# Two tables of weight sums instead of three in the second MLP of a decoder trunk, with the fourth block added on VectorE

## The chip, the core and the metric

The kernel runs on one core of one Trainium2 chip. The metric is the time of one execution on the device in microseconds (us), the median over runs. All data is float32 in memory. TensorE multiplies float32 data here as pairs of float32r halves ("hi" and "lo", three products for each float32 product), so every weight block first goes through ScalarE (the hi half, a copy to float32r) and VectorE (the lo half, what the copy left over).

Names of the engines as in the profile: PE is TensorE, PEld its weight loads, ACT is ScalarE, DVE is VectorE, POOL is GpSimd, SP is SyncE. SP and POOL here do almost nothing but issue DMA transfers; a transfer that adds to what stands at its target (an "accumulation" below) is issued by POOL in this kernel.

## The reference, cut to what matters

Two layers over 512 tokens of width 1024. Layer 0 is attention (16 heads) and an MLP, layer 1 a gated short convolution and an MLP. The MLP is the part the change works on:

```python
def conv_ffn(h, norm_g, w_up, conv_w, w_down):
    xn = rms_norm(h, norm_g)
    u = causal_dwconv(xn @ w_up, conv_w)          # w_up: 1024 x 5632
    g, val = u[..., :D_FF], u[..., D_FF:]         # D_FF = 2816
    return (jax.nn.silu(g) * val) @ w_down

def reference(x, ...):
    h = x
    for layer in range(2):
        mixer = attention_mixer if layer % 2 == 0 else short_conv_mixer
        h = h + mixer(h, ...)
        h = h + conv_ffn(h, ffn_norm[layer], ffn_w_up[layer], ffn_conv[layer], ffn_w_down[layer])
    return h
```

## The kernel before, in words

The program runs in stages, one after another on PE: attention, its output projection, the first MLP (up, then down), the input projection of the convolution mixer, its output projection, the second MLP (up, then down).

**Seven products instead of eight.** Most of the up projections and the input projection of the convolution are done as 2x2 block products in seven products rather than eight (`Sevens`). The weight of a group `g` of 256 columns is cut into four blocks of 512 rows: lower or upper half of the rows, gate or value columns. The seven products are named `p1 p7 p3 p6 p2 q5 q4`, and each of them takes one block or a sum of blocks as its weight. One product is 24 matmuls of 256 columns (`seven`). `slot(g, s)` issues slot `s` of group `g`: one product on PE, and around it the weight halves on ACT and DVE (`weights_of`), the loads for later slots on SP (`load_pair`, `load_one`), the accumulations on POOL (`add_block`). `p1` takes the block `X`; after its halves are made, `first_sums` lets POOL add another block to `X` in place, and `q5` takes that sum. `p2` takes the block `W`, `p3` the block `Z`, `p7` the buffer `Y`.

**Tables.** In the two MLPs three of the weights are sums over two, three and four blocks. They are not summed on chip: `table_steps` writes them beforehand as tables `t` in device memory. A table `7` is one block plus a second, a table `6` is table `7` plus a third, a table `4` is table `6` plus the fourth. Nine groups are cut into three pieces (`CHUNKS`), each piece into two halves of its rows; for each half the steps run copy, add, copy, add, copy, add, each of 768 KB. That is 36 transfers for a layer, all issued by POOL. An add waits for the copy before it, a copy from table to table waits for the add before it, and such a wait stands on POOL: whatever is behind it in POOL's queue stands too. The line of the adds is L101, that of the copies L104. `Y` is loaded from table `7`, `p6` takes table `6` and `q4` table `4`.

The list of 36 steps is a generator that the program draws from at fixed places; `FAR` says how many steps are drawn where. The order on POOL is the program's (`pin`). For layer 1: 9 steps behind the attention, 9 ahead of the convolution's first `first_sums`, 18 behind its slot 20 (the last accumulation into `Xc` is in that slot). A tile name with a `c` at its end (`Xc`, `Yc`) belongs to the convolution's seven products, which use accumulations instead of tables.

**Plain part and chores.** In each up projection groups 0 and 1 (`PLAIN = 2`) are done as plain products with 512 columns, and group 2 (`base`) is the first one of the seven-product form. What is left of the plain groups and of the preparation of the inputs is put into a list of chores for DVE and ACT; `up.rate` says how many microseconds of it (by the program's own estimate) are let go in a slot.

The instructions of PE, ACT and DVE are put in order by a scheduler in the framework; loads with a table, the halves on ACT and all transfers on POOL are held in the program's order.

Of the kernel before, what the change touches and what calls it, by code (L numbers as in the profile page):

```python
# [22 lines left out]
ALU = mybir.AluOpType  # L23
# [23 lines left out]
FILL1, FILL2, BEFORE = 1.5, 3.3, 2.0  # L47
UNITS = (0, 1), (2,), (3,)
PLAIN = 2
FAR = 9, 9, 18  # L50
CHUNKS = (2, 3), (5, 3), (8, 3)
SHARE = 0.58

# [2 lines left out]
def trunk(  # L56
# [7 lines left out]
    act, dve, pe, pool = nc.scalar, nc.vector, nc.tensor, nc.gpsimd  # L64
# [12 lines left out]
    def bank(tag):  # L77
        n_ps[0] += 1
        return ps.tile([P, S], F32, tag=tag, name=f"ps{tag}{n_ps[0]}", bufs={"a": 2, "b": 4, "c": 2}[tag])
# [6 lines left out]
    def table_steps(layer):  # L86

        w = ffn_w_up[layer]
        for n in "764":
            for g, m in CHUNKS:  # L90
                tables[layer, n, g] = far.tile([512, m * 256 + 16], F32, tag=f"t{layer}{n}{g}", name=f"t{layer}{n}{g}")
        def block(kh, half, g, m):
            return w[kh * 512:(kh + 1) * 512, half * DFF + g * 256:half * DFF + (g + m) * 256]
        for g, m in CHUNKS:
            for rows in (slice(0, 256), slice(256, 512)):
                for step in range(6):
                    n = "764"[step // 2]
                    to = tables[layer, n, g][rows, 0:m * 256]
                    if step % 2:
                        src = block(*((0, 1), (0, 0), (1, 0))[step // 2], g, m)  # L100
                        pin(nc.gpsimd.dma_start(to, src[rows, :], accum_op=ALU.add))  # L101
                    else:
                        src = block(1, 1, g, m) if step == 0 else tables[layer, "76"[step // 2 - 1], g][:, 0:m * 256]
                        pin(nc.gpsimd.dma_start(to, src[rows, :]))  # L104
                    yield

    def table_of(layer, n, group):
        g, m = next(c for c in CHUNKS if c[0] <= group < c[0] + c[1])
        return tables[layer, n, g][:, (group - g) * 256:(group - g + 1) * 256].rearrange("(k p) c -> p k c", p=P)
# [197 lines left out]
    def weights(ahead=AHEAD):  # L307
        fetch(1 + ahead)
        at[0] += 1
        return ready[at[0] - 1]  # L310
# [23 lines left out]
    class Norm:  # L334
# [3 lines left out]
        def __init__(self, name, base):  # L338
            self.name, self.base = name, base
            self.row, self.held, self.first = None, [], True  # L340
            self.acc = own.tile([P, S], F32, tag="nrow", name=f"nacc_{name}", bufs=1) if name != "n0" else None
# [135 lines left out]
    def products(acc, w, order=tuple(range(ND))):  # L477
        for k in order:
            yield mm3(acc, (w[0][:, k, :], w[1][:, k, :]), hs(k), k == order[0], k == order[-1])
# [486 lines left out]

    run(sums_far)
    sums_far = table_steps(1)

    def sum_far(n):  # L970
        for _ in range(n):
            next(sums_far, None)

    sum_far(FAR[0])

# [84 lines left out]
    class Sevens:  # L1060

        def __init__(self, name, mp, groups, block_of):
            self.name, self.mp, self.groups, self.block_of = name, mp, groups, block_of
            self.forms = {n: [mp.tile([P, 4, HT], F32R, tag=f"{n}_{i}", name=f"{n}_{i}{name}") for i in ("hi", "lo")] for n in FORMS}
            self.st, self.wides, self.table = {}, {}, None

        def load_pair(self, g):
            s = self.st[g] = {}
# [40 lines left out]
        def first_sums(self, g):  # L1109
            self.weights_of(g, "p7", "Y")  # L1110
            if not self.table:
                dve.tensor_tensor(self.st[g]["Y"], self.st[g]["Y"], self.st[g]["X"], op=ALU.add)
            self.add_block(g, "X", 0, 1)
            if self.table:
                self.load_one(g, "p6 sum", self.table("6", g))

        def open_wides(self, g):
            self.wides[g] = self.wides_of(g)
# [7 lines left out]
        def slot(self, g, s):  # L1126

            on, was, soon = (i in self.groups for i in (g, g - 1, g + 1))
            if self.chores:
                self.work_off(self.rate(g, s))  # L1130
            form, n, fresh = (("p1", "A", True), ("p7", "T", True), ("p3", "R", False), ("p6", "R", False), ("p2", "A", False),
                              ("q5", "R", False), ("q4", "T", False))[s]
            if s == 2:
                if was:
                    self.product(g - 1, form, n, fresh)
            elif on:
                self.product(g, form, n, fresh)
            st, p, c = self.st, g - 1, self.st.get(g)
            if s == 0:
                if was:  # L1140
                    if "p3" not in st[p]:
                        self.weights_of(p, "p3", "Z")
                    self.join(p, "yg", st[p]["T"], st[p]["Xs"])
                if on:
                    self.load_one(g, "W", self.block_of(g, 1, 0))
                if soon:
                    self.load_pair(g + 1)
            elif s == 1:
                first = not was
                if on and first and not self.ahead:  # L1150
                    self.weights_of(g, "p6", "p6 sum" if self.table else "Y")
                if on:
                    act.activation(self.bank_of(g, "R"), c["A"], AF.Copy, scale=-1.0)
                if on and not first:
                    self.weights_of(g, "p6", "p6 sum" if self.table else "Y")
                if soon and not self.table:
                    self.add_block(g + 1, "Y", 1, 1)
            elif s == 2:
                if on:
                    self.kept(g, "P7s", c["T"])  # L1160
                    self.weights_of(g, "p2", "W")
                    if self.table:
                        self.load_one(g, "q4 sum", self.table("4", g))
                    else:
                        dve.tensor_tensor(c["Y"], c["Y"], c["W"], op=ALU.add)
            elif s == 3:
                if was:
                    self.early(p, st[p]["R"])
                if on:
                    self.weights_of(g, "q5", "X")  # L1170
            elif s == 4:
                if on:
                    self.kept(g, "Xs", c["R"])
                    self.weights_of(g, "q4", "q4 sum" if self.table else "Y")
            if was and s != 2:
                self.tail(p, s)
            if s == 5:
                if on:
                    self.load_one(g, "Z", self.block_of(g, 1, 1))
                    self.open_wides(g)  # L1180
                    self.left(g, c["A"])
                if soon:
                    self.weights_of(g + 1, "p1", "X")
                elif on and self.ahead:
                    self.weights_of(g, "p3", "Z")
            elif s == 6:
                if on:
                    self.join(g, "yv", c["R"], c["P7s"])
                if soon:
                    self.first_sums(g + 1)  # L1190
# [17 lines left out]
    def up_seven(layer, norm, mp):  # L1208

        blocks = Blocks(mp, layer)  # L1210
        w_up, base = ffn_w_up[layer], PLAIN
# [5 lines left out]
        up = Sevens(layer, mp, range(base, HF), block_of)  # L1217
        up.norm, up.chores = norm, []
        up.table = lambda n, g: table_of(layer, n, g)
        up.rate = lambda g, s: 1.4 if g == base else 0.5  # L1220

        def wides_of(g):
            if g == base - 1:
# [78 lines left out]
    def conv_seven(norm, mp):  # L1302
# [5 lines left out]
        up = Sevens("c", mp, range(1, 5), block_of)  # L1308
# [98 lines left out]
        def gate(o, acc):  # L1407
            dve.tensor_tensor(early_b[:, o, :], acc, norm.row, op=ALU.mult)
            yield 0.69

        accs = []
        for j in range(8):
            accs.append(bank("bbbbaabb"[j]))
            for _ in products(accs[-1], weights(), (4, 5, 6, 7, 0, 1, 2, 3)):
                up.work_off(SHARE)
            if j in (1, 3):
                chores.append(input_(j // 2, *accs[j - 1:]))
            if j == 3:
                chores.append(prepare())
            if j >= 4:  # L1420
                chores.insert(0, gate(j - 4, accs[j]))
            if j == 5:
                up.load_pair(1)
                up.add_block(1, "Y", 1, 1)
                sum_far(FAR[1])
            if j == 7:
                up.weights_of(1, "p1", "X")
                up.first_sums(1)
                up.weights_of(1, "p6", "Y")
        want_conv_out()  # L1430
        for s in range(28):
            up.slot(1 + s // 7, s % 7)
            if s == 20:
                sum_far(FAR[2])
            if s == 27:
                fetch(1)
# [251 lines left out]
```

## Time and profile before

| what | value |
|---|---|
| three runs, us | 1143.35, 1142.93, 1141.8 (median 1142.93) |
| profiled execution, us | 1142.31, its span 1140.5 |
| PE busy | 1117.3 us (98% of the span), 7691 matmuls |
| DVE busy | 932.6 us (82%), ACT 679.0 us (60%), POOL 167.9 us (15%) |
| DMA | 223.51 MB, mean 196 GB/s |

The profiled execution took 0.62 us less than the median of the three runs, and 1.8 us of its time lie outside its span. PE is busy nearly everywhere, so a change can bring time only where PE stands still or where its clock is lowered, and cost time only where it makes PE stand. Shares of the whole span say little: what counts is, for each product, which of its operands came last, and whether PE had to wait for it. In us from the start of the span, the attention's last matmuls start at 255, the seven-product groups of the first MLP run on PE from 324 to 513, those of the convolution from 662 to 744, those of the second MLP from 834 to 1034, each behind its plain part, and the second MLP's down projection ends the program.

### The profile page before, as it was taken

The page shows a single profiled execution, that of the slowest core. Times are in us where ns is not written, and L with a number is a line of the kernel's source. Part 1 is how long each engine was busy: PE and PEld are TensorE (multiplying, and loading weights), DVE is VectorE, ACT ScalarE, POOL GpSimd, SP SyncE. Part 2 cuts the span into 40 slices and gives each one's busy share as a digit, 9 for nine tenths or more (in the row PEclk, how much of TensorE's full clock was granted, in tenths as well). Part 3 has the DMA queues.
Part 4 walks back from the last instruction along what each step waited for, and adds up shares of the span by engine and source line. Part 5 has one row for each costly group of instructions (what it writes and reads, how often), then busy time and mean ns, then how long its engine had stood idle before and what let it go on. Part 6 is the DMA issues. An engine that isn't in the chain of part 4 may idle for free.

```text
span 1140.5 us, 19427 instructions
## 1 busy us (share of the span) xinstructions
PE 1117.3 (98%) x7691; PEld 1010.5 (89%) x7691; DVE 932.6 (82%) x1430; ACT 679.0 (60%) x1013; POOL 167.9 (15%) x203
## 2 busy tenths in 40 slices
PE   8999999999999999999999999999969999999998
PEld 7888787878889999999999799988869999998886
DVE  6787888887889887888978988865968788788886
ACT  7556676745567666676556354543545666666553
POOL 4011111111011110024201111111111110014300
PEclk9999999999999999999999999999989999999999
DMA  6678778677888786799957967689886968799961
GB/s 192 180 173 205 164 182 200 162 204 194 214 213 213 194 215 179 198 315 195 225 158 181 233 151 159 143 228 235 241 185 178 220 173 211 204 251 228 230 158 56
DMA packets 182940, 223.51 MB, mean 196 GB/s; under 512 B 7900, under 2 KB 145164, under 8 KB 182848
## 3 DMA queue, kind: packets, MB, share of 16 engines
q0 software_dynamic: 43520, 96.38, 42.5%
q1 hardware_dynamic: 139168, 125.81, 35.5%
q8 instruction: 60, 0.98, 0.3%
q14 instruction: 32, 0.26, 0.1%
q10 hardware_dynamic: 160, 0.07, 0.0%
HBM read 217.26 MB, written 58.72 MB: 242 GB/s over the span
## 4 chain that ended last, share of the span: by engine, by line
PE 71%; DMA 12%; DVE 9%; issue 4%; ACT 3%; POOL 0%; DVEq 0%; SPq 0%; ACTq 0%; POOLq 0%
PE psb L1055 22%; PE psb L1600 10%; PE psa L1055 8%; PE psa L1600 8%; DMA t<-in_ffn_w_up 5%; PE psb L314 3%; PE psb L315 3%; PE psb L316 3%; DMA t<-t 2%; DMA Xc<-in_conv_w_in 2%; DMA X<-in_ffn_w_up 2%; PE psb L689 1%; PE psa L785 1%; PE psa L314 1%; PE psa L316 1%
## 5 line engine op out<-in xcount | busy, mean ns | idle before, releaser
L293 ACT ACTIVATE whi<-raw 128x1024 fp32r<-128x1024 f32 (+2 forms) x89 | 91.6, 1031 | 94.4 <-PE psb L315 26.0
L294 DVE TENSOR_TENSOR wlo<-raw,whi 128x1024 fp32r<-128x1024 f32 (+2 forms) x89 | 105.5, 1186 | 26.3 <-ACT whi L293 25.4
L1055 PE MATMUL psb<-p_lo,whi_p 128*128 128x256 f32 x432 | 121.6, 281 | 0.0
L1055 PE MATMUL psb<-p_hi,wlo_p 128*128 128x256 f32 x432 | 121.6, 281 | 0.0
L1055 PE MATMUL psb<-p_hi,whi_p 128*128 128x256 f32 x432 | 121.2, 281 | 0.0
L314 PE MATMUL psb<-hs_a,whi 128*128 128x512 f32 x224 | 92.2, 412 | 0.0
L1055 PE MATMUL psb<-q_hi,whi_q 128*128 128x256 f32 x288 | 81.2, 282 | 10.5 <-ACT Xs L1107 10.5
L316 PE MATMUL psb<-hs_a,wlo 128*128 128x512 f32 x224 | 88.7, 397 | 0.0
L1055 PEld LDWEIGHTS psb<-p_hi,whi_p 128*128 128x128 f32 x432 | 81.9, 190 | 0.0
L1055 PE MATMUL psa<-p_hi,wlo_p 128*128 128x256 f32 x288 | 81.9, 284 | 0.0
L1055 PE MATMUL psa<-p_lo,whi_p 128*128 128x256 f32 x288 | 81.8, 284 | 0.0
L1055 PE MATMUL psa<-p_hi,whi_p 128*128 128x256 f32 x288 | 81.6, 283 | 0.0
L1055 PEld LDWEIGHTS psb<-p_lo,whi_p 128*128 128x128 f32 x432 | 81.3, 188 | 0.0
L1055 PEld LDWEIGHTS psb<-p_hi,wlo_p 128*128 128x128 f32 x432 | 81.2, 188 | 0.0
L1055 PE MATMUL psb<-q_lo,whi_q 128*128 128x256 f32 x288 | 81.2, 282 | 0.0
L1055 PE MATMUL psb<-q_hi,wlo_q 128*128 128x256 f32 x288 | 81.0, 281 | 0.0
L101 POOL DMA_DIRECT2D t<-in_ffn_w_up x36 | 33.0, 916 | 222.0 <-DMA t<-t 121.9
L1055 PEld LDWEIGHTS psb<-q_hi,whi_q 128*128 128x128 f32 x288 | 54.7, 190 | 10.9 <-ACT Xs L1107 10.9
L1600 PE MATMUL psb<-act,whi 128*128 128x256 f32 x352 | 63.1, 282 | 0.1
L424 DVE SCALAR_TENSOR_TENSOR uv<-yv,taps,uv 128x511 f32<-128x511 f32 (+1 forms) x80 | 56.6, 745 | 0.0
L1600 PE MATMUL psb<-whi,act 128*128 128x512 f32 x176 | 56.3, 397 | 0.0
L424 DVE SCALAR_TENSOR_TENSOR ug<-yg,taps,ug 128x511 f32<-128x511 f32 (+1 forms) x80 | 55.6, 746 | 0.0
(475 smaller groups left out, 3644.8 us busy)
## 6 DMA issues: line engine op xcount, KB each, us to landing
t<-in_ffn_w_up POOLq DMA_DIRECT2D x48, 768.0 KB, 8.3
t<-t POOLq DMA_DIRECT2D x24, 768.0 KB, 5.0
raw<-in_attn_w_in SPq DMA_DIRECT2D x24, 512.0 KB, 5.1
X<-in_ffn_w_up SPq DMA_DIRECT2D x18, 512.0 KB, 5.1
Y<-t SPq DMA_DIRECT2D x18, 512.0 KB, 6.2
p6 sum<-t SPq DMA_DIRECT2D x18, 512.0 KB, 3.9
W<-in_ffn_w_up SPq DMA_DIRECT2D x18, 512.0 KB, 4.1
q4 sum<-t SPq DMA_DIRECT2D x18, 512.0 KB, 5.7
```

What stands on the lines that cost most here:

```text
L101: pin(nc.gpsimd.dma_start(to, src[rows, :], accum_op=ALU.add))
L293: return (act.activation(hi[:, at_], raw[:, at_], AF.Copy), dve.tensor_tensor(lo[:, at_], raw[:, at_], f32(hi[:, at_]), op=ALU.subtract))
L294: dve.tensor_tensor(lo[:, at_], raw[:, at_], f32(hi[:, at_]), op=ALU.subtract))
L314: made = [pe.matmul(acc, w[0], rhs[0], start=first, stop=False), pe.matmul(acc, w[0], rhs[1], start=False, stop=False), pe.matmul(acc, w[1 ...
L315: pe.matmul(acc, w[0], rhs[1], start=False, stop=False),
L316: pe.matmul(acc, w[1], rhs[0], start=False, stop=last)]
L424: dve.scalar_tensor_tensor(dst[:, d:], src[:, 0:S - d], tap(j), dst[:, d:], op0=ALU.mult, op1=ALU.add)
L689: pe.matmul(ss[e][:, c:c + wide], ql[rows, b * P:n], kl[rows, 0:wide], start=first and b == bs[0], stop=last and b == bs[-1])
L785: pe.matmul(out_, w, t[:, first:first + step * (NB - k - 1) + 1:step, :], start=k == 0 and i == 0, stop=k == NB - 1 and i == 1)
L1055: pe.matmul(to, w[a][:, k, c], x[b][:, k, :], start=fresh and i + k + t == 0, stop=i == 1 and k == 3 and t == 2, skip_group_check=not fresh)
L1600: pe.matmul(to, l, r, start=begin and o + t == 0, stop=end and t == 2 and o == (0 if layer else 1), skip_group_check=not fresh)
```

## The change

In layer 1 the table `4` is not written: 24 transfers stand in place of 36, and the nine loads of 512 KB from that table on SP go too. The sum of four blocks is made on DVE, in slot 2 of each group, as table `6`'s block (now named `three`) plus `W`, in place. The draws are placed anew: 7 steps behind the attention, one each behind slots 1, 8 and 15 of the convolution (right behind the accumulation into the next group's `Yc`), 14 behind slot 20. The rate of chores in the second MLP's groups behind the first is 0.3 instead of 0.5. Layer 0 keeps its three tables.

```diff
-FAR = 9, 9, 18
+FAR = 7, 1, 14
 ...
-        for n in "764":
+        for n in "76" if layer else "764":
 ...
-                for step in range(6):
+                for step in range(4 if layer else 6):
 ...
             if self.table:
-                self.load_one(g, "p6 sum", self.table("6", g))
+                self.load_one(g, "three", self.table("6", g))
 ...
                 if on:
                     self.kept(g, "P7s", c["T"])
                     self.weights_of(g, "p2", "W")
-                    if self.table:
-                        self.load_one(g, "q4 sum", self.table("4", g))
+                    if self.fours:
+                        self.load_one(g, "four", self.table("4", g))
                     else:
-                        dve.tensor_tensor(c["Y"], c["Y"], c["W"], op=ALU.add)
+                        c["four"] = c["three" if self.table else "Y"]
+                        dve.tensor_tensor(c["four"], c["four"], c["W"], op=ALU.add)
 ...
-        up.rate = lambda g, s: 1.4 if g == base else 0.5
+        up.fours = layer == 0
+        up.rate = lambda g, s: 1.4 if g == base else 0.3 if layer else 0.5
 ...
             if j == 5:
                 up.load_pair(1)
                 up.add_block(1, "Y", 1, 1)
-                sum_far(FAR[1])
 ...
         for s in range(28):
             up.slot(1 + s // 7, s % 7)
-            if s == 20:
+            if s in (1, 8, 15):
+                sum_far(FAR[1])
+            elif s == 20:
                 sum_far(FAR[2])
```

POOL's queue in the convolution's input projection, before (`Yc` and `Xc` are accumulations into the buffers of the weights, `t` are table steps):

```order
L1082 DMA Yc_7655<-in_conv_w_in 128x4x256
L101 DMA t_3286<-in_ffn_w_up 256x768
L104 DMA t_3289<-t_3286 256x768
L101 DMA t_3289<-in_ffn_w_up 256x768
L104 DMA t_3284<-in_ffn_w_up 256x768
L101 DMA t_3284<-in_ffn_w_up 256x768
L104 DMA t_3287<-t_3284 256x768
L101 DMA t_3287<-in_ffn_w_up 256x768
L104 DMA t_3290<-t_3287 256x768
L101 DMA t_3290<-in_ffn_w_up 256x768
L1082 DMA Xc_7654<-in_conv_w_in 128x4x256
```

The same place with the change:

```order
L1082 DMA Yc_7650<-in_conv_w_in 128x4x256
L1082 DMA Xc_7649<-in_conv_w_in 128x4x256
L1082 DMA Yc_7762<-in_conv_w_in 128x4x256
L101 DMA t_3286<-in_ffn_w_up 256x768
L1082 DMA Xc_7761<-in_conv_w_in 128x4x256
L1082 DMA Yc_7957<-in_conv_w_in 128x4x256
L104 DMA t_3284<-in_ffn_w_up 256x768
L1082 DMA Xc_7956<-in_conv_w_in 128x4x256
L1082 DMA Yc_8191<-in_conv_w_in 128x4x256
L101 DMA t_3284<-in_ffn_w_up 256x768
L1082 DMA Xc_8190<-in_conv_w_in 128x4x256
```

Nine table steps in a row ahead of the first `Xc` became single ones behind the `Yc` of groups 2, 3 and 4. Behind the last `Xc` there follow 18 steps before and 14 now, and then the second MLP's first accumulation into `X`.

DVE in group 2 of the second MLP, before (`p6 sum` is table 6's block, `whi` and `wlo` are the halves of a weight, `hs_a_wide` and `head` belong to chores):

```order
L1005 TENSOR_TENSOR wlo_p_9414<-p6 sum_9340,whi_p_9413 128x1024
L1042 TENSOR_TENSOR head_8980<-ug_9107,uv_9108 128x256
L1043 SCALAR_TENSOR_TENSOR head_8980<-ug_9107,uv_9108 128x256
L1271 TENSOR_TENSOR hs_a_wide_9431<-psb_9227,nrow_n_9085 128x512
L1271 TENSOR_TENSOR hs_a_wide_9431<-psc_9271,nrow_n_9085 128x512
L1271 TENSOR_TENSOR hs_a_wide_9431<-psc_9306,nrow_n_9085 128x512
L424 SCALAR_TENSOR_TENSOR hs_a_wide_9431<-hs_a_wide_9431,taps 128x511 x2
L424 SCALAR_TENSOR_TENSOR hs_a_wide_9431<-hs_a_wide_9431,taps 128x510 x2
L1005 TENSOR_TENSOR wlo_p_9422<-W_9379,whi_p_9421 128x1024
L1005 TENSOR_TENSOR wlo_q_9458<-X_9267,whi_q_9457 128x1024
```

The same place with the change:

```order
L1005 TENSOR_TENSOR wlo_p_9399<-three_9325,whi_p_9398 128x1024
L1042 TENSOR_TENSOR head_8965<-ug_9092,uv_9093 128x256
L1166 TENSOR_TENSOR three_9325<-three_9325,W_9364 128x1024
L1043 SCALAR_TENSOR_TENSOR head_8965<-ug_9092,uv_9093 128x256
L1273 TENSOR_TENSOR hs_a_wide_9415<-psb_9212,nrow_n_9070 128x512
L1273 TENSOR_TENSOR hs_a_wide_9415<-psc_9256,nrow_n_9070 128x512
L1273 TENSOR_TENSOR hs_a_wide_9415<-psc_9291,nrow_n_9070 128x512
L424 SCALAR_TENSOR_TENSOR hs_a_wide_9415<-hs_a_wide_9415,taps 128x511 x2
L1005 TENSOR_TENSOR wlo_p_9407<-W_9364,whi_p_9406 128x1024
L1005 TENSOR_TENSOR wlo_q_9442<-X_9252,whi_q_9441 128x1024
```

The add (L1166) stands ahead of the lo half of `W`, and two chore instructions of 510 columns moved behind the lo half of `X`. In the later groups it also stands between the halves of `three` and of `W`.

PE in the same group, before (`psa` with `p_hi` and `p_lo` is product `p2`, `psb` with `q_hi` and `q_lo` is product `q5`, `ident,h` are transposes for the residual):

```order
L1055 MATMUL psa_9354<-p_hi_8989,whi_p_9421 128x256
L1055 MATMUL psa_9354<-p_lo_8990,whi_p_9421 128x256
L1525 MATMUL psc_11757<-ident,h 128x128 x4
L1055 MATMUL psb_9417<-q_hi_8991,whi_q_9457 128x256
L1055 MATMUL psb_9417<-q_lo_8992,whi_q_9457 128x256
L1055 MATMUL psa_9354<-p_hi_8989,wlo_p_9422 128x256
L1055 MATMUL psa_9354<-p_hi_8989,whi_p_9421 128x256
```

The same place with the change:

```order
L1055 MATMUL psa_9339<-p_hi_8974,whi_p_9406 128x256
L1055 MATMUL psa_9339<-p_lo_8975,whi_p_9406 128x256
L1528 MATMUL psc_11733<-ident,h 128x128 x4
L1055 MATMUL psa_9339<-p_hi_8974,wlo_p_9407 128x256
L1055 MATMUL psa_9339<-p_hi_8974,whi_p_9406 128x256
L1055 MATMUL psa_9339<-p_lo_8975,whi_p_9406 128x256
```

Before, the first two matmuls of `q5` stand in front of the other 22 of `p2`; now `p2` is issued whole and `q5` follows it. This is the only place at which PE's order differs.

More of the change, by code (lines that the diff above doesn't have):

```diff
@@ L1064, in __init__ @@
             self.forms = {n: [mp.tile([P, 4, HT], F32R, tag=f"{n}_{i}", name=f"{n}_{i}{name}") for i in ("hi", "lo")] for n in FORMS}
-            self.st, self.wides, self.table = {}, {}, None
+            self.st, self.wides, self.table, self.fours = {}, {}, None, False
         def load_pair(self, g):
@@ L1150, in slot @@
                 if on and first and not self.ahead:
-                    self.weights_of(g, "p6", "p6 sum" if self.table else "Y")
+                    self.weights_of(g, "p6", "three" if self.table else "Y")
                 if on:
@@ L1154, in slot @@
                 if on and not first:
-                    self.weights_of(g, "p6", "p6 sum" if self.table else "Y")
+                    self.weights_of(g, "p6", "three" if self.table else "Y")
                 if soon and not self.table:
@@ L1173, in slot @@
                     self.kept(g, "Xs", c["R"])
-                    self.weights_of(g, "q4", "q4 sum" if self.table else "Y")
+                    self.weights_of(g, "q4", "four")
             if was and s != 2:
```

## The prediction

> **What bounds the kernel now.** I read the page's busy times and slices first, then who PE waited for, then the chain of waits around the longest wait, then PE, POOL and DVE in order of time there.
>
> ```profile
> PE 1117.3 (98%) x7691; PEld 1010.5 (89%) x7691; DVE 932.6 (82%) x1430; ACT 679.0 (60%) x1013; POOL 167.9 (15%) x203
> PE   8999999999999999999999999999969999999998
> ```
>
> PE is idle for 1140.5 - 1117.3 = 23.2 us of the span, and one slice stands out: a 6 among nines. The list of whom PE waited for gives it a name:
>
> ```profile
> PE psb L1055 <- ACT Xs L1107: 10.5, 2, 9.4
> PE psb L1055 <- ACT Xsc L1107: 0.6, 1, 0.6
> PE psa L1055 <- DVE wlo_p2c L1005: 0.3, 1, 0.3
> ```
>
> One wait of 9.4 us stands out, of a matmul in a seven-product group for ACT's copy `Xs`; the other 1.1 of its row is a second case, and the rest is small. The chain around it (us from the start, us, what):
>
> ```profile
> 839.88 11.58 DMA X<-in_ffn_w_up
> ...
> 852.51 0.59 ACT Xs L1107
> ```
>
> ACT is only the messenger. The wait is for the accumulation into `X` of group 2 in the second MLP: it was issued at 839.88, right behind a table step, and landed 11.58 us later. Was it late because of POOL, or because `X` was not free sooner? The instructions around it, in order of time, the second MLP and then the same places of the first:
>
> ```profile
> 829.77 1.22 DVE L1005 TENSOR_TENSOR wlo_p<-X,whi_p 128x1024 fp32r<-128x1024 f32 x1
> 834.34 0.28 PE L1055 MATMUL psa<-p_hi,whi_p 128*128 128x256 f32 x1
> 839.32 0.87 POOL L101 DMA_DIRECT2D t<-in_ffn_w_up  x1 [5.72 <-DMA t<-t]
> 839.88 1.67 POOL L1082 DMA_DIRECT2D X<-in_ffn_w_up  x1
> 843.12 0.60 PE L1525 MATMUL psc<-ident,h 128*128 128x128 f32 x4
> 853.14 0.58 PE L1055 MATMUL psb<-q_hi,whi_q 128*128 128x256 f32 x1 [9.42 <-ACT Xs L1107]
> 866.31 0.28 PE L1055 MATMUL psb<-p_hi,whi_p 128*128 128x256 f32 x1
> 321.84 0.58 POOL L104 DMA_DIRECT2D t<-t  x1 [7.62 <-DMA t<-in_ffn_w_up]
> 323.66 1.35 POOL L1082 DMA_DIRECT2D X<-in_ffn_w_up  x1 [1.24 <-DVE wlo_p L1005]
> 324.07 0.28 PE L1055 MATMUL psa<-p_hi,whi_p 128*128 128x256 f32 x1
> 336.73 0.39 PE L1055 MATMUL psb<-q_hi,whi_q 128*128 128x256 f32 x1 [1.05 <-ACT Xs L1107]
> 345.36 0.28 PE L1055 MATMUL psb<-p_hi,whi_p 128*128 128x256 f32 x1
> ```
>
> DVE had read `X` by 829.77 + 1.22 = 830.99. In the first MLP POOL waits for just that (1.24 us <- wlo_p) and issues; in the second it waits for table steps (5.72 us <- t) until 839.3. The table costs the accumulation 8.9 us.
>
> **What the stall costs, all told.** From a group's `p1` to the next group's `p1` there are seven products; from the first `p1` of group 2 to the first `p7` of group 3 there are seven too, as group 2 has no `p3` behind it. Undisturbed, seven products take, from one later group's `p2` to the next one's,
>
> ```profile
> 874.99 2.84 PE psa L1055 x24
> ...
> 894.87 2.85 PE psa L1055 x24
> ```
>
> 19.88 us. The second MLP took 866.31 - 834.34 = 31.97, of which four transposes are about 0.35. So 31.97 - 20.23 = 11.7 us are lost: 9.42 of waiting, and the rest because the clock was halved afterwards (columns: us, PE busy and its matmuls, granted clock, DMA share, GB/s):
>
> ```profile
> 853.14:857.50 4.36, 4.36 (x20) 0.50 0.21 50
> ```
>
> Twenty matmuls in 4.36 us, where 2.84/24 x 20 = 2.4 is normal: 2.0 us. The first MLP took 345.36 - 324.07 = 21.29, so 1.4 us were lost there.
>
> **The change part by part.**
>
> *Fewer steps behind slot 20.* The waits and issue times of the 18 steps, grouped by line:
>
> ```profile
> L101 POOL DMA_DIRECT2D t<-in_ffn_w_up x9 | 7.9, 874 | 60.9 <-DMA t<-t 35.8 <-DMA t<-in_ffn_w_up 25.1
> L104 POOL DMA_DIRECT2D t<-t x6 | 3.5, 591 | 41.1 <-DMA t<-in_ffn_w_up 41.1
> L104 POOL DMA_DIRECT2D t<-in_ffn_w_up x3 | 2.9, 975 | 0.0
> 724.46 1.15 POOL L104 DMA_DIRECT2D t<-in_ffn_w_up  x1
> ```
>
> An add behind a table copy waits 35.8/6 = 6.0 us, an add behind a copy of weights 25.1/3 = 8.4, a table copy 41.1/6 = 6.9. The 14 steps are a table copy and its add, then three times copy, add, table copy, add; the first finds its source landed. Waits: 4 x 6.0 + 3 x (8.4 + 6.9) = 69.9; issue 7 x 0.87 + 4 x 0.59 + 3 x 0.98 = 11.4. The last step is issued at 724.5 + 81 = 806, and is down by 815. The accumulation can go at 831.0, with 25 us to spare.
>
> *What is late next there.* PE now does `p2` whole before `q5`. `q5` is due at 834.34 + 4 x 2.84 + 0.35 = 846.05. How long the accumulation takes, by the page's median of its kind and by the first MLP's chain, and two kinds of DVE work before `q5`:
>
> ```profile
> X<-in_ffn_w_up POOLq DMA_DIRECT2D x18, 512.0 KB, 8.0
> 323.66 10.79 DMA X<-in_ffn_w_up
> L424 DVE SCALAR_TENSOR_TENSOR ug<-yg,taps,ug 128x511 f32<-128x511 f32 (+1 forms) x80 | 55.6, 746 | 0.0
> 842.21 1.22 DVE L1005 TENSOR_TENSOR wlo_p<-W,whi_p 128x1024 fp32r<-128x1024 f32 x1
> ```
>
> At 8.0 us it lands at 839, at 10.79 or 11.58 at 841.8 or 842.6. PE went on 853.14 - 851.46 = 1.7 us after the landing; each of the three leaves that much before 846.05. On DVE the add (1.22, as the lo halves, whose shape it has) comes ahead of the lo half of `W`, and two chore instructions of 0.75 have moved behind that of `X`. So `W`'s half starts at about 842.21 + 1.22 - 1.49 = 841.9 and ends at 843.2. `p2`'s third matmul wants it after the transposes, at 843.12 + 0.35 = 843.5. That is a narrow fit, and I leave 0.3 us for it. Gain of the second MLP: 11.7 - 0.3 = 11.4 us.
>
> *Seven steps behind the attention.* The table copy at 321.84, in flight when the first MLP's accumulation went, comes about two steps (15 us) sooner. That accumulation took 10.79 us instead of 8.0, and its stall costs 1.4 us in all. Bounds: 0 and 1.4. I take 0.8, since loads by SP remain in flight there.
>
> *Single steps in the convolution.* Here three transfers of 768 KB come beside transfers that PE nearly waits for. The tightest, in the chain and in order of time:
>
> ```profile
> 669.26 7.56 DMA Xc<-in_conv_w_in
> 678.01 1.23 DVE L1005 TENSOR_TENSOR wlo_p1c<-Xc,whi_p1c 128x1024 fp32r<-128x1024 f32 x1 [2.87 <-ACT whi_p1c L1003]
> 680.19 0.28 PE L1055 MATMUL psa<-p_hic,wlo_p1c 128*128 128x256 f32 x1
> ```
>
> It is SP's load of group 2's `X`. Its lo half is done at 679.24, 0.95 us before PE takes it. It runs beside POOL's accumulation into `Yc`, behind which the table step now stands. On the other side the nine steps ahead of the first `Xc` are gone, which frees the loads before this one. Bounds: a gain of 0.9 (the waits of 0.6 and 0.3 above vanish) and a cost of 4.2 - 0.95 = 3.3 (half of an add's 8.4 us falls on that load). I take a cost of 0.2, near the gain's end, as POOL's row was busy there before.
>
> The Trainium skill (DMA: Bandwidth & Descriptors, Queues, rings and completion order) has a rule that speaks against this placing: each DMA engine takes packets from the queue rows in turn. By it SP's load shares the engines with POOL's row as long as that row has work, and the row has work longer now. No run here shows yet how much of it falls on this load; the rival below prices it from the rows above.
>
> *The add on DVE.* Nine adds of 1.22 us, 11 us in all. In seven groups of the second MLP (880 to 1017) DVE waits at the very place where the add goes, ahead of the lo half of `W`:
>
> ```profile
> L1005 DVE TENSOR_TENSOR wlo_p<-W,whi_p 128x1024 fp32r<-128x1024 f32 x7 | 8.6, 1226 | 10.4 <-ACT whi_p L1003 10.4
> ```
>
> 10.4/7 = 1.5 us a group, for ACT's half. Price zero; without that cover, up to 1.22 us a group, 11 us. The lower rate of chores moves a few chores of groups 1 and 2 one or two slots later; price zero.
>
> *The loads.* Nine loads fewer on SP. But `three` now keeps its buffer until `q4`'s halves are made, so the next group's `three` is issued later, and `W` and `X` queue behind it on SP. It is the one new wait, priced below as a rival.
>
> Sum against the profiled execution: 1142.31 - 11.4 - 0.8 + 0.2 = 1130.3. The median of the runs is 0.6 higher than that execution, which by the same difference of 12.0 gives 1130.9. I forecast 1130.6.
>
> **The rivals.**
>
> *The convolution pays.* SP's load at 669.26 is held up by half of a step, 3.3 us beyond what it has to spare, and the places in the next two groups by up to 0.9 each: 1 to 5 us over the 0.2 taken, so 1131.6 to 1135.6. For it: a spare time below a microsecond. Against: POOL's row was not empty there before. By the page's rule above it is this case that comes true.
>
> *The late `three`* makes it slower than before. The last reader of `three` in a group is the lo half for `q4`:
>
> ```profile
> 916.65 1.22 DVE L1005 TENSOR_TENSOR wlo_q<-q4 sum,whi_q 128x1024 fp32r<-128x1024 f32 x1
> 926.11 8.52 PE psb L1055 x72
> 926.64 1.05 ACT L1003 ACTIVATE whi_p<-p6 sum 128x1024 fp32r<-128x1024 f32 x1
> DMA to landing us min/median/max: 3.6/3.9/9.3
> ```
>
> The load can go at 917.9. PE begins `p6` at 926.11 + 2 x 2.84 = 931.8, and the halves take 1.05 + 1.22 = 2.3, so it may land 11.6 us after its issue. Beyond that PE stands in eight groups; from 11.6 + 12/8 = 13.1 us on the whole gain is gone, and at 14.5 the time is 1130.3 + 8 x 2.9 = 1153.5. Against it: the last row, the landings of that load before, has 9.3 as its longest, and `three` is the first of the loads that go at that moment.
>
> *It doesn't do what it says.* If the accumulation were held by DVE rather than by the table, nothing would change: 1142. The 830.99 above speaks against it.
>
> **How the numbers follow.** Forecast 0.80: 1128.6 (all of 1.4 and 0.9 gained, no loss at `p2`: 1142.31 - 11.7 - 1.4 - 0.9 = 1128.3, with the median's 0.6 half) to 1132.3 (nothing gained in the first MLP, 0.9 lost in the convolution). The convolution pays: 0.11. The late `three`: 0.05, of which 0.01 ends within the gain. No effect: 0.04. The range goes from 1128.3 to 1135.0, which takes in most of the first rival and leaves out the others. A difference of 0.2%, 2.3 us, is about what a measurement of this kernel can tell from no change. Faster 0.92, within it 0.04, slower 0.04.
>
> **What would show it right or wrong.** In the profile after: the last table step on POOL near 806 and the accumulation into `X` at about 831, with "<- DVE wlo_p" as its releaser; no wait for `Xs` above 0.5 us in the second MLP and a granted clock of 1.00 there; 20.2 to 20.6 us from `p1` to `p7` there; the waits for `Xsc` in the convolution below 2 us; DVE's wait ahead of the lo half of `W` down from 1.5 to 0.3 us. I would be wrong if PE waited in every group from 860 on, or if the convolution's groups took over 19.9 us each.

## The result, and the profile after

The changed kernel takes 1131.24 us in the median of five runs (1130.97 to 1134.2), against 1142.93 us (1141.8 to 1143.35) for the kernel before beside it: a ratio of 0.9905, 95% interval 0.989 to 0.9919. The forecast was 1130.6, range 1128.3 to 1135.0. The profiled execution took 1132.23 us, its span 1130.0.

The page of the changed kernel, busy times and PE's slices:

```profile
PE 1116.2 (99%) x7691; PEld 1009.3 (89%) x7691; DVE 942.9 (83%) x1439; ACT 680.0 (60%) x1013; POOL 159.3 (14%) x191
PE   8999999999999999999999999999999999999998
```

The 6 among the nines is gone. PE is idle for 1130.0 - 1116.2 = 13.8 us, where it was 23.2. DVE is 10.3 us busier and has nine instructions more (the adds), POOL has twelve instructions fewer. Whom PE waited for in this execution (us in total, times, longest):

```profile
PE psa L1055 <- ACT whi_p1c L1003: 1.8, 1, 1.8
PE psa L1055 <- DVE wlo_p1c L1005: 1.0, 2, 0.8
PE psb L1055 <- ACT Xsc L1107: 0.6, 1, 0.6
```

No wait for `Xs` is left, in either MLP. New at the head of the list is a wait that is not among the signs the prediction set, though one of its rivals priced it: for the first product of a group in the convolution. POOL, DVE and PE around the old stall, each in order of time, then DVE's group that answers to the wait of 1.5 us a group before, and PE in the stretch from group 2's `p1` to group 3's `p7` (its length, PE busy and its matmuls, granted clock, DMA share, GB/s):

```profile
808.11 0.88 POOL L101 DMA_DIRECT2D t<-in_ffn_w_up  x1 [4.71 <-DMA t<-t]
831.84 1.33 POOL L1082 DMA_DIRECT2D X<-in_ffn_w_up  x1 [22.85 <-DVE wlo_p L1005]
837.96 1.23 DVE L1166 TENSOR_TENSOR three<-three,W 128x1024 f32<-128x1024 f32 x1
842.55 1.24 DVE L1005 TENSOR_TENSOR wlo_p<-W,whi_p 128x1024 fp32r<-128x1024 f32 x1
834.89 0.28 PE L1055 MATMUL psa<-p_hi,whi_p 128*128 128x256 f32 x1
844.02 0.36 PE L1055 MATMUL psa<-p_hi,wlo_p 128*128 128x256 f32 x1
855.24 0.28 PE L1055 MATMUL psb<-p_hi,whi_p 128*128 128x256 f32 x1
L1005 DVE TENSOR_TENSOR wlo_p<-W,whi_p 128x1024 fp32r<-128x1024 f32 x7 | 8.6, 1226 | 1.6 <-ACT whi_p L1003 1.6
834.89:855.24 20.35, 20.35 (x174) 1.00 0.74 165
```

The last table step of the row goes at 808.11 (forecast 806), and POOL then stands idle for 22.85 us until DVE has read `X`: the releaser is DVE now, no longer the table. From group 2's `p1` to group 3's `p7` are 855.24 - 834.89 = 20.35 us, where it was 31.97 (forecast 20.2 to 20.6), at a granted clock of 1.00. DVE's wait ahead of the lo half of `W` went from 10.4 us in seven groups to 1.6: the add has filled it.

### The profile page after: what moved, and what is told of

Read it like the earlier page. It is cut to its first block, busy times and chain, and to the rows that moved or that the text cites. A ratio compares the mean times of both kernels' runs of the same rounds, so it can differ in the third digit from the quotient of the medians.

```text
span 1130.0 us, 19403 instructions
## 1 busy us (share of the span) xinstructions
PE 1116.2 (99%) x7691; PEld 1009.3 (89%) x7691; DVE 942.9 (83%) x1439; ACT 680.0 (60%) x1013; POOL 159.3 (14%) x191
## 4 chain that ended last, share of the span: by engine, by line
PE 87%; DVE 5%; DMA 3%; issue 2%; ACT 2%; DVEq 0%; ACTq 0%; POOLq 0%
PE psb L1055 25%; PE psb L1603 10%; PE psa L1055 10%; PE psa L1603 6%; PE psb L314 5%; PE psb L315 5%; PE psb L316 5%; PE psa L316 2%; PE psa L314 2%; PE psa L315 2%; DMA Xc<-in_conv_w_in 2%; PE psa L785 2%; PE psb L689 2%; DMA raw<-in_ffn_w_down 1%; DVE wlo L294 1%
## 5 line engine op out<-in xcount | busy, mean ns | idle before, releaser
L1603 PEld LDWEIGHTS psb<-act,whi 128*128 128x128 f32 x352 | 54.2, 189 | 0.5 <-DVE act L1005 0.3
L1055 PEld LDWEIGHTS psa<-p_hi,whi_p 128*128 128x128 f32 x288 | 54.5, 189 | 0.1
```

The source lines that it names most:

```text
L1055: pe.matmul(to, w[a][:, k, c], x[b][:, k, :], start=fresh and i + k + t == 0, stop=i == 1 and k == 3 and t == 2, skip_group_check=not fresh)
L1603: pe.matmul(to, l, r, start=begin and o + t == 0, stop=end and t == 2 and o == (0 if layer else 1), skip_group_check=not fresh)
```

## The experiments

The experiments ran in three sets, each on a chip of its own and each with the kernel before beside it: first three_tables, blocked, row_of_three and none_in_conv, then after_again, add_twice, add_four and both_two, then three_none, none_again and nine_first. There the kernel before took 1145.0 to 1145.3 us in the median (single runs 1140.5 to 1149.8), some 2 us more than beside the result, so between sets ratios are compared, and times only within a set.

**What made the gain: place, or fewer transfers?** Theory Q says the queue on POOL, rival B the bytes, rival O the order on PE. *three_tables* gives the kernel before nothing but another place for four steps:

```diff
-FAR = 9, 9, 18
+FAR = 9, 9, 14
...
             self.add_block(g, "X", 0, 1)
             if self.table:
+                if g in (4, 5) and self.name == 1:
+                    sum_far(2)
```

> The kernel before with all its 36 steps, its three tables, its loads and its order on PE; only the last four of the 18 steps behind slot 20 are drawn later, two each behind the accumulations into X of groups 4 and 5 of the second MLP. Theory Q (the gain is POOL's queue being free when group 2's accumulation wants to go): 14 steps at 115/18 = 6.4 us end near 814, the accumulation is issued at 831 and the wait of 9.4 us goes; 11.4 us gained, about 1131.5. Rival B (the gain is fewer transfers and bytes, 12 steps and nine loads): nothing changes, 1142.9. Rival O (the gain is PE's order, p2 whole ahead of q5): nothing changes either, 1142.9, as the order on PE is that of before.

Measured: 1130.97 us, ratio to the kernel before 0.9877 (0.9857 to 0.9896). POOL in its trace:

```profile
812.32 0.88 POOL L101 DMA_DIRECT2D t<-in_ffn_w_up  x1 [9.64 <-DMA t<-in_ffn_w_up]
829.62 1.33 POOL L1082 DMA_DIRECT2D X<-in_ffn_w_up  x1 [16.42 <-DVE wlo_p L1005]
```

With all 36 steps, all loads and the old order on PE the accumulation waits for DVE alone, and the whole gain is there (the changed kernel has 0.9886 in the second set). B and O fall: neither the bytes nor PE's order made it, and as this run has the old rate of chores too, nor did that.

*blocked* goes the other way: two tables, but 20 steps behind slot 20.

```diff
-FAR = 7, 1, 14
+FAR = 1, 1, 20
```

> The changed kernel with its 24 steps dealt 1 behind the attention, 1 three times, and 20 behind slot 20. Theory Q: at 81/14 = 5.8 us a step the last is issued at 724.5 + 116 = 840, as in the kernel before, and the accumulation into X right behind it lands near 850; q5 is due at 846, so PE waits some 6 us for Xs (2.6 us less than before, since p2 is issued whole first) and loses 2 us more of the clock: 1139 to 1141. Rival B: as many bytes as the changed kernel, so 1131.2, no change. Rival O: the order on PE is that of the changed kernel, so 1131.2.

Measured: 1151.96 us, ratio 1.0071 (1.0047 to 1.0095). POOL, the wait on PE, and a stretch after it (its length, the busy time of PE, PE's weight loads, DVE, ACT and POOL, the granted clock, DMA share, GB/s):

```profile
724.77 1.18 POOL L104 DMA_DIRECT2D t<-in_ffn_w_up  x1
851.73 1.67 POOL L1082 DMA_DIRECT2D X<-in_ffn_w_up  x1
863.53 0.58 PE L1055 MATMUL psb<-q_hi,whi_q 128*128 128x256 f32 x1 [16.54 <-ACT Xs L1107]
862.00:866.00 4.00, 2.47 (x11) 2.47 (x12) 3.43 (x4) 4.00 (x8) 0.00 (x0) 0.50 0.01 1
```

The accumulation went at 851.73, and PE waited 16.54 us for it and went on at a clock of 0.50. The stall is back with the bytes and the order on PE of the changed kernel, so Q stands. It is larger than expected, because the row took longer: 851.73 - 724.77 = 127 us for 20 steps, 6.35 each, not the 5.8 taken (which is the prediction's 81/14; in the changed kernel those 14 took 84 us, 6.0 each, the first of them with its source landed). The row ended nearly 12 us later than worked out, and the time is 11 us above the upper end of what was expected: while PE waits for the row, what the row is late by is lost.

**What the single steps in the convolution cost.** Theory S: a step beside SP's load of group 2's `Xc` holds that load up. Rival A: the load is slow because it now goes earlier, beside POOL's accumulation into `Yc`, step or not. *row_of_three* puts the three steps in a row where nine stood before; *none_in_conv* (the second diff) moves them behind slot 20.

```diff
-FAR = 7, 1, 14
+FAR = 7, 3, 14
...
                 up.add_block(1, "Y", 1, 1)
+                sum_far(FAR[1])
...
-            if s in (1, 8, 15):
-                sum_far(FAR[1])
-            elif s == 20:
+            if s == 20:
```

```diff
-FAR = 7, 1, 14
+FAR = 7, 1, 17
...
-            if s in (1, 8, 15):
-                sum_far(FAR[1])
-            elif s == 20:
+            if s == 20:
```

> The changed kernel with the three single steps of the convolution in one row ahead of the first accumulation into Xc (where nine stood before), 600 to about 620. Theory S (a table step beside SP's load of group 2's Xc holds that load up): the load takes 7.6 us again instead of 11.45, PE's waits for whi_p1c and wlo_p1c at the start of group 2 (1.8 and 0.8) go, 2.6 us gained, 1128.6; up to 1.4 us of it may be lost where the row lies beside the last loads of the plain part. Rival A (the load is slow because it now goes 3 us earlier, beside POOL's accumulation into Yc, step or not): the waits stay, 1131.2.

> The changed kernel with no step in the convolution: 7 behind the attention, 17 behind slot 20. Theory S: the load of group 2's Xc takes 7.6 us, 2.6 us gained, 1128.6. Theory Q: 17 steps at 5.8 us end with an issue at 823.6, still ahead of 831, so the accumulation into X is not held up; no wait for Xs. Rival A: the waits at the start of group 2 stay, 1131.2. Rival R (a step in flight beside the accumulation into X slows it, as in the first MLP of the kernel before, 10.8 us instead of 8.0): it lands at 841.8, still 4 us ahead of q5 at 846, so nothing.

Measured: row_of_three 1129.18 us, 0.9866 (0.9846 to 0.9886); none_in_conv 1128.94 us, 0.986 (0.984 to 0.988). The load in the changed kernel, with what hangs on it and with the time that the step took to land (last line, 13.8 us), and then the load and the first product of the same group in row_of_three:

```profile
663.64 2.06 POOL L101 DMA_DIRECT2D t<-in_ffn_w_up  x1
666.18 11.45 DMA Xc<-in_conv_w_in
677.71 1.06 ACT L1003 ACTIVATE whi_p1c<-Xc 128x1024 fp32r<-128x1024 f32 x1 [5.72 <-DMA Xc<-in_conv_w_in]
678.82 0.39 PE L1055 MATMUL psa<-p_hic,whi_p1c 128*128 128x256 f32 x1 [1.78 <-ACT whi_p1c L1003]
680.08 0.39 PE L1055 MATMUL psa<-p_hic,wlo_p1c 128*128 128x256 f32 x1 [0.76 <-DVE wlo_p1c L1005]
t<-in_ffn_w_up POOLq DMA_DIRECT2D x1, 768.0 KB, 13.8
```

```profile
667.46 7.24 DMA Xc<-in_conv_w_in
678.15 0.28 PE L1055 MATMUL psa<-p_hic,whi_p1c 128*128 128x256 f32 x1
```

The load takes 7.24 us without the step and 11.45 with it. In the traces of all kernels here it takes 7.2 to 7.7 us where no step stands behind that accumulation (7.56 in the kernel before) and 10.7 to 11.6 in the five that have the step there (11.56 in blocked). In row_of_three it goes nearly as early as in the changed kernel (667.46), beside the same accumulation into `Yc`, and is fast. So S holds and A falls: the step costs the load some 4 us, and PE 1.78 + 0.76 = 2.5.

The Trainium skill (DMA: Bandwidth & Descriptors, Queues, rings and completion order) says that each DMA engine serves the queue rows that have work in turn. By it a step of 768 KB in POOL's row takes turns with SP's load. The trace agrees in so far as the load takes 11.45 us beside the step and 7.24 without. The turns alone do not give this size: in the kernel before, too, POOL's row had work for nearly all of the load, as the accumulation into `Yc` was in flight from 666.04 to 676.0, and the load, from 669.26 to 676.82, took only 7.56. What all thirteen traces show is when the load ends: within 1 us of the landing of the last transfer in POOL's row, which without the step is that accumulation, and with it the step (663.64 + 13.8 = 677.4 in the changed kernel, where the load lands at 677.63). Why it takes until then stays open.

*after_again* is the changed kernel once more, beside the runs of the second set.

> The changed kernel itself, unaltered, timed beside the runs of this set on their chip. Every theory: 1131 to 1133, the ratio to the kernel before about 0.990; the load of group 2's Xc takes 11 to 12 us again and PE waits some 2.6 us at the start of that group.

Measured: 1131.36 us, 0.9886 (0.9865 to 0.9907), the load 11.47 us, the waits 1.8 and 0.8.

**Is the add on VectorE free?** *add_twice* and *add_four* make the same sum two and four times; the line shown stands once in the first and three times in the second.

```diff
                         c["four"] = c["three" if self.table else "Y"]
+                        if self.table:
+                            dve.tensor_tensor(c["Y"], c["four"], c["W"], op=ALU.add)
                         dve.tensor_tensor(c["four"], c["four"], c["W"], op=ALU.add)
```

> The changed kernel with the add of three and W done twice in each of the nine groups (the first sum goes to a buffer that nobody reads any more): 1.22 us more of VectorE a group, at the place of the add. Theory C (the add lies in time that VectorE waits through): in a steady group VectorE still waits 2.7 us, 1.4 of them right behind, and the lo half of W is done 2.7 us before the matmul that reads it, so nothing is lost, the time of the changed kernel. Rival D (VectorE's work there is on the path): 9 x 1.22 = 11 us slower, 1142.

> The same with four adds a group in place of one: 3.7 us more of VectorE a group. Theory C: that is 1.0 us beyond the 2.7 us that it waits in a steady group, and 0.7 us beyond what the lo half of W has to spare, so 0.7 to 1.0 us a group in eight or nine groups, 6 to 9 us slower than the changed kernel. Rival D: 33 us slower. Rival N (VectorE never matters): no change.

Measured: add_twice 1132.24 us, 0.9892 (0.9871 to 0.9913), 0.9 us over after_again, less than the interval tells apart; add_four 1140.58 us, 0.9959 (0.9944 to 0.9975), 9.2 us slower than after_again, just above the 6 to 9 worked out. The group of DVE's halves of `X` in 880 to 1017, with the wait ahead of it, in the changed kernel, in add_twice and in add_four:

```profile
L1005 DVE TENSOR_TENSOR wlo_q<-X,whi_q 128x1024 fp32r<-128x1024 f32 x7 | 8.6, 1225 | 9.8 <-ACT whi_q L1003 9.8
```

```profile
L1005 DVE TENSOR_TENSOR wlo_q<-X,whi_q 128x1024 fp32r<-128x1024 f32 x7 | 8.6, 1225 | 7.6 <-ACT whi_q L1003 7.6
```

```profile
L1005 DVE TENSOR_TENSOR wlo_q<-X,whi_q 128x1024 fp32r<-128x1024 f32 x7 | 8.5, 1220 | 0.2 <-ACT whi_q L1003 0.2
```

The first extra add eats into the waiting, three use it up: of these 137 us DVE is busy for 120.3, 127.5 and 135.2. Theory C holds and D falls: DVE has cover for the change's one add, and about one more, not for four. In add_four two products `p2` that lie four groups apart stand at

```profile
909.06 2.84 PE psa L1055 x24
...
991.27 2.84 PE psa L1055 x24
```

82.21 us, or 20.55 a group in place of 19.88: the 0.7 that was worked out.

**Is there more in fewer transfers?** *both_two* is none_in_conv with two tables in the first MLP too.

```diff
-        for n in "76" if layer else "764":
+        for n in "76":
...
-                for step in range(4 if layer else 6):
+                for step in range(4):
...
-        up.fours = layer == 0
```

> The changed kernel with 7 steps behind the attention, none in the convolution and 17 behind slot 20, and two tables in the first MLP as well, the sum of four blocks being made by VectorE in both. Theory Q: the first MLP's accumulation into X has waited for no step since the change, so there is nothing left to gain from fewer transfers there: the time of the version with three tables there, 1129 or 0.986 of the kernel before. Rival B (fewer transfers and bytes are worth something by themselves): 12 steps and nine loads fewer once more, 2 us or more faster than that. Rival D: 11 us slower.

Measured: 1128.57 us, 0.986 (0.9834 to 0.9886), the same ratio as none_in_conv. No gain shows from twelve steps and nine loads fewer where no queue is waited for; the intervals would leave room for one of 2 us or so.

**Then why drop the third table at all?** *three_none* asks whether three tables could have the better placing too.

```diff
-FAR = 9, 9, 18
+FAR = 9, 0, 15
...
+                if g in (3, 4, 5, 6) and self.name == 1:
+                    sum_far(3)
```

> The kernel before (three tables, 36 steps, all loads, its order on PE) with no step in the convolution: 9 steps behind the attention, 15 behind slot 20, and three each behind the accumulations into X of groups 3 to 6 of the second MLP. Theory P (all of the gain is a matter of where the steps stand, none of the third table): the same time as the changed kernel without steps in the convolution, within 1 us. Rival K (the third table costs something wherever its steps stand): three steps of 6.4 us between accumulations 19.9 us apart fill POOL's row, so accumulations into X come late or land slowly, 1 us or more in some of groups 4 to 7: 2 to 4 us slower than that version, 1131 to 1133.

*none_again*, the two-table version of that placing, ran beside it:

> The changed kernel with 7 steps behind the attention, none in the convolution and 17 behind slot 20, once more, timed beside the two above: about 1129, 0.986 of the kernel before.

Measured: 1147.77 us, 1.0022 (1.001 to 1.0034), against 1129.0 for none_again (0.9855, 0.9832 to 0.9877). PE's wait and POOL in the trace of three_none:

```profile
PE psb L1055 <- ACT Xs L1107: 13.7, 5, 8.1
891.38 0.88 POOL L101 DMA_DIRECT2D t<-in_ffn_w_up  x1 [4.58 <-DMA t<-t]
893.79 2.90 POOL L1082 DMA_DIRECT2D X<-in_ffn_w_up  x1
894.55 2.75 POOL L104 DMA_DIRECT2D t<-in_ffn_w_up  x1
912.33 0.58 PE L1055 MATMUL psb<-q_hi,whi_q 128*128 128x256 f32 x1 [8.07 <-ACT Xs L1107]
```

Theory P falls. Rival K named the groups and the mechanism, but its price was far too low: the accumulations go behind late steps and land beside others, and groups 4 to 7 stall. Four of the five waits, 13.1 us, are theirs (the fifth is in the first MLP). Against none_again the products behind them stand 19.2 us later; the rest goes as PE runs on slower after a wait, at a granted clock of 0.67 from 912 to 917 us and 0.79 from 930 to 940. So the third table is harmless where its steps have room (three_tables: nine in a row ahead of the convolution's first `Xc`, and two a group later), and three a group have no room. Whether another placing outside the convolution would hold all 36 was not tried; dropping the table makes the room without one.

**The first MLP's 1.4 us.** *nine_first* is none_in_conv with nine steps behind the attention, as before the change, and 15 behind slot 20.

```diff
-FAR = 7, 1, 17
+FAR = 9, 1, 15
```

> The changed kernel with no step in the convolution, 9 steps behind the attention in place of 7, and 15 behind slot 20. Theory F (the first MLP lost 1.4 us before only in those executions in which the ninth step, a table copy then, was still in flight when the accumulation into X went): the ninth of these is a copy of weights, issued between 305 and 322; if it has landed by 323.7 the accumulation takes 8 us and nothing is lost, otherwise it takes near 10.8 us and PE waits near 1 us for Xs. So 0 to 1.4 us slower than with 7 steps. Rival G (the stall there was there by the number of steps, whatever their speed): 1.4 us slower in any case.

Measured: 1128.85 us, 0.985 (0.9833 to 0.9867), against 1129.0 for none_again; the interval alone could not tell 1.4 us, the trace can. Its ninth step and the accumulation after it, then the same two in three_tables, whose program up to there is that of the kernel before:

```profile
310.61 0.89 POOL L104 DMA_DIRECT2D t<-in_ffn_w_up  x1
323.32 1.35 POOL L1082 DMA_DIRECT2D X<-in_ffn_w_up  x1 [11.82 <-DVE wlo_p L1005]
```

```profile
313.39 0.58 POOL L104 DMA_DIRECT2D t<-t  x1 [6.62 <-DMA t<-in_ffn_w_up]
323.63 1.35 POOL L1082 DMA_DIRECT2D X<-in_ffn_w_up  x1 [9.65 <-DVE wlo_p L1005]
```

In both the accumulation waits for DVE alone, and PE does not wait for `Xs`. The ninth step that was issued at 321.84 in the profiled run of the kernel before was issued 8 us sooner in three_tables. three_none, the same program up to there once more, had it late again:

```profile
322.80 0.58 POOL L104 DMA_DIRECT2D t<-t  x1 [9.17 <-DMA t<-in_ffn_w_up]
323.40 1.36 POOL L1082 DMA_DIRECT2D X<-in_ffn_w_up  x1
```

There PE waited 0.6 us for `Xs`. Theory F holds: the stall belongs to the executions in which the row runs late, not to the number of steps.

## Why the prediction was right, point by point

*The second MLP: right.* 11.4 us forecast; 31.97 - 20.35 = 11.6 gained in the profile. The last step, the releaser, the missing wait and the length of the stretch are as written. The narrow fit at `p2`, priced at 0.3, held: the lo half of `W` was done at 842.55 + 1.24 = 843.79, and the matmul that reads it went at 844.02, behind four transposes that hide it. three_tables and blocked show the mechanism from both sides.

*The first MLP: the term was 0.8, the profile shows 1.24*, as PE's products behind the stall stand that much earlier (three products of a later group at 384.03 for 385.27). nine_first, three_tables and three_none show that the stall comes and goes with the pace of the steps.

*The steps gone ahead of the convolution: a term left out.* The prediction bounded the gain at 0.9, the waits of 0.6 and 0.3 within the convolution's groups, and had nothing for PE's waits ahead of them. In the profile the convolution's first product starts at 659.59 for 662.21, 2.6 us sooner: 1.24 from the first MLP, and the rest because two waits of PE ahead of it are gone, which in the kernel before read

```profile
577.73 0.39 PE L1600 MATMUL psa<-act,whi 128*128 128x256 f32 x1 [0.66 <-DVE act L1007]
631.02 0.65 PE L374 MATMUL psc<-ident,ncol_n 128*128 128x128 f32 x4 [0.65 <-DVE ncol_n L412]
```

That the second went with the traffic of the nine steps is likely: three_tables, which keeps them there, still has 0.5 of it, and row_of_three, with three, has none. The first is gone in three_tables too, so it is not the steps', and its cause stays open.

*The convolution: the step that failed.* "I take a cost of 0.2, near the gain's end, as POOL's row was busy there before." From the convolution's first product to the second MLP's, the kernel before took 834.34 - 662.21 = 172.1 us, the changed kernel 834.89 - 659.59 = 175.3. So 3.2 us were lost, close to the bound of 3.3 that the sum had and did not take. Instruction by instruction, the changed kernel gained 0.5 more up to group 2, lost 3.1 at that group's first product (2.5 of it the two waits) and 0.6 at group 3's, where PE waited 0.27; as row_of_three has 0.41 of waiting there, that last part need not be the single step's. The rival "The convolution pays" named the load, the mechanism and half of a step (4.2 us; 3.9 to 4.2 measured against row_of_three and the kernel before). The time it gave, 1131.6 to 1135.6, was not reached, because what was gained ahead of the convolution was not in it. Its argument against was wrong: the accumulation into `Yc` was in POOL's row before too, but the load lands with the end of that row, and with the step behind the accumulation the row ends at 677.4. row_of_three takes the step away and the load is back at 7.24. Of the sign "if the convolution's groups took over 19.9 us each" two in three came: from one first product to the next they took 19.2, 21.1 and 21.5 us, where the kernel before had 17.75, 19.9 and 21.05.

*So the total was right partly because two errors met.* 1.8 us more gained ahead of the convolution, 3.0 more lost in it and 0.2 more gained in the second MLP leave 0.9 against the forecast. In the profiled execution 0.7 more went behind all that, where the chain runs through a load for the down product,

```profile
1078.82 7.78 DMA raw<-in_ffn_w_down
```

that is not in the chain of the kernel before and that no experiment touched, and 0.4 more lies outside the span (2.2 us for 1.8). The sum gave 1130.3, and with 0.9, 0.7 and 0.4 it is 1132.3; the execution took 1132.23. The measured median, 1131.24, falls into the prediction's main branch, 1128.6 to 1132.3, in which the convolution loses 0.9 us at most, although it lost 3.2: that is luck. One figure of that branch does not come out as written: with nothing gained in the first MLP and 0.9 lost the sum gives 1131.8, 1132.1 with half of the median's 0.6, not 1132.3; nothing hangs on it.

*The add and the late `three`: right.* No price of the one add shows, and add_four shows where it would begin. `three`, said to be safe up to 11.6 us, landed within

```profile
DMA to landing us min/median/max: 3.5/3.7/5.1
```

of its issue. The lower rate of chores was not tried by itself; nothing in the profile asks for a price other than zero.

*A better version.* With no step in the convolution the kernel takes 1128.9 us (none_in_conv, none_again and nine_first: 1128.94, 1129.0, 1128.85), 0.985 to 0.986 of the kernel before, where the changed kernel has 0.9886 in after_again. The intervals of these ratios overlap. Within one set, both_two, which has that placing too, took 1127.26 to 1130.4 us and after_again 1130.56 to 1133.73, and the traces show where the time comes from: the waits of 1.8 and 0.8 are gone.

## What to carry to other kernels

A long background job on an in-order queue was paid for here not by its bytes but by what stood behind it in the queue and what landed beside it: both_two drops twelve transfers with no gain that shows, three_tables gains all that the change gains by moving four. So work out when the queue must be empty, and then look, as here at the load of group 2's `Xc`, for the tightest transfer on another queue that the moved job will now lie beside. Give a pacing that you read from one execution some room: 5.8 us a step was worked out from the kernel before, and 6.0 and 6.35 were measured.

## What had not been expected of the hardware

The same chain of dependent transfers ran at a pace that differed from one execution to the next. The ninth step behind the attention was issued at 321.84, 313.39 and 322.80 us in three executions of the same instructions up to there (the kernel before, three_tables, three_none); whether the chip or the execution makes the difference stays open. A cycle of four steps behind slot 20 took 24.7 us twice in the changed kernel and between 24.2 and 28.0 in the first four of blocked. And a load of 512 KB that took 7.2 to 7.7 us beside an accumulation took 10.7 to 11.6 when a transfer of 768 KB was queued behind that accumulation on the other engine's queue: in all thirteen traces it landed about when the last transfer on that queue did.
